# Fewer and later bias-row writes, half-size x loads for the squares, and shifted attention tasks in a hybrid decoder layer

## The chip, the cores and the metric

The kernel runs on one core of a Trainium2 chip. The metric is device microseconds (us) of one execution; the time before is the median of three runs.

## The reference

One layer: RMS norm of x (256 tokens by 4096), one input projection to 16384 columns, two token mixers, a gate on each, one output projection, a residual sum and a final RMS norm. With 256 tokens the attention has a single block per head, so it is plain causal attention with a bias that depends on the distance of query and key:

```python
u = rmsnorm(h, norm_gain)
q, k, v, z_a, hc, b_gate, c_gate, z_c = split(u @ w_in)      # 2048 columns each
logits = q @ k.T * 128 ** -0.5 + bias_tab[head, rel_bucket(i - j)]   # 16 heads x 128, j <= i
attn = softmax(logits) @ v * silu(z_a)
conv = b_gate * short_conv(c_gate * hc, conv_w) * silu(z_c)  # causal, width 3
h = h + concatenate([attn, conv]) @ w_out
out = rmsnorm(h, final_gain)
```

## The kernel before, in words

**The work in quads.** Weights stream through the core once. The 256 tokens are two halves of 128, columns are taken in pairs of 512-wide chunks, and the 4096 rows of a weight in 16 *quads* of 256 rows. A pair of chunks goes through 16 quads; there are 16 pairs for the input projection (p = 0 to 15) and four for the output projection (p = 16 to 19), so 320 quads. Each quad is one transfer of 1 MB into a buffer named raw. The 2 by 2 block product of a quad is done either in the usual way, with 8 block products (24 matmuls of 128x512), or, for quads 0, 2, 4, 6, 8 and 10, with 7 products of sums and differences (21 matmuls; "seven" quads below). Every operand is split into a high and a low part for accuracy: ACT casts `hi` (L472), DVE takes `lo` as the rest (L473), PE does hi x hi, hi x rest and lo x hi (L529 to L531). A seven quad also needs three sums on DVE (L461 to L463).

**Buffers and look-ahead.** raw has three buffers and is loaded two quads ahead (L435), all from SP's queue; hi and lo are rings of three, so that the splits run at most two units ahead of PE (a unit is half of a usual quad or a third of a seven quad).

**The first pair.** In p = 0 the x operands are also made. For each quad an x piece `xr` of 256 KB is loaded (L121), scaled with the norm's gain and split (L137 and L138, or for a seven quad L129, L113, L116 and L117). The order of quads in this pair (the list FIRST) has four usual quads first; then seven and usual quads alternate. In between lie three side jobs:

- `bias_rows` (called behind the third quad, i = 2): the bias table and a one-hot matrix are loaded (L188, L190), one matmul (L192) makes one row of 384 bias values per head, DVE copies it (L194), and one transfer (L195) writes each row 128 times to a scratch tensor in DRAM, `bias_d`.
- `squares` (i = 6 to 9): a quarter of x in row layout is loaded in two halves of 512 KB (L159), and ACT sums the squares (L160), for the RMS norm. The buffers have the tags "v" and "z".
- `token_scale` (i = 11) makes the factors of the norm, and `bias_load` fetches the bias tiles of heads 0 and 1. The rows of a bias tile are the same row shifted by one element each, which a stride of 383 over the copies in DRAM gives (L206, L208: two transfers of 128 partitions per head).

**End of a pair.** When the last seven quad of a pair is done, four of its sums are complete: `early` reads them out (L313 to L317, L580). After the last quad `two_done` (L328) writes the results: q and k after an even pair, v and z after an odd one.

**Attention tasks.** Groups of four heads are worked in between the block products of the following pairs. From the last seven quad of a pair on, the block products are counted, and a table (`tasks_of`) says after which count a task is emitted, and in which PSUM bank: `turn` (transposes of q and k, L216, copied by ACT, L218), `scores` (L223, L224, the bias added by DVE, L226, the softmax), `probs` (transposes, L240) in the odd pairs 1, 3, 5, 7; `values` and `mixed` in the even pairs 2 to 8; `conv` in pairs 10, 12, 14. `scores` of head h also calls `bias_load(h + 2)`, since there are two bias tiles. SP issues its DMAs strictly in the order in which they stand in its queue, and a DMA that has to wait for a buffer holds up all behind it. What stands in which place is decided by a scheduler; the order is the same in each execution.

Of the kernel before, what the change touches and what calls it, by code (L numbers as in the profile page):

```python
# [10 lines left out]
F32 = mybir.dt.float32  # L11
F32R = mybir.dt.float32r
BF16 = mybir.dt.bfloat16
AF = mybir.ActivationFunctionType
# [3 lines left out]
P = 128  # L18
S = 256
# [3 lines left out]
H = 16  # L23
HG = 4
NDP = 4
# [3 lines left out]
B = 512  # L29
# [3 lines left out]
RING = 3  # L33
LEAD = 2
BUCKETS = 32

EDGES = [16, 19, 21, 24, 27, 31, 35, 40, 46, 52, 59, 67, 77, 87, 99, 113]

# [21 lines left out]
def hymba_layer(ctx: ExitStack, tc: tile.TileContext, xT, xres, gain, w, convw, wout,  # L60
                relb, onehot, fgain, out):
    nc = tc.nc
    PSUM = bass.MemoryType.PSUM
    ps_ = ctx.enter_context(tc.tile_pool(name="ps", bufs=1, space=PSUM))
    dram = ctx.enter_context(tc.tile_pool(name="dram", bufs=1, space=bass.MemoryType.DRAM))
# [9 lines left out]
    sx = const.tile([P, 2, NDP], F32, name="sx")  # L75
    ss = const.tile([P, 2, 2 * NDP], F32, name="ss")
    const.tile([P, 8], F32, name="pad")
    bias_d = dram.tile([H, P, 384], F32, name="bias_d")
    m_d = dram.tile([NQ, P, 4 * P], F32, name="m_d")

    kt = ctx.enter_context(tc.tile_pool(name="kt", bufs=1, side="left"))
# [3 lines left out]
    pool = right.enter_context(tc.tile_pool(name="attn", bufs=1, side="right"))  # L85
    cur = {"pool": pool}

    def bank(n):
        return ps_.tile([P, 512], F32, name=f"p{n}")
# [62 lines left out]
            parts(dst, c[:, :4])  # L152


    def squares(p):
        for t in range(2):
            xq = pool.tile([P, 2, B], F32, name="xq", tag="vz"[t])
            xq = xq.rearrange("p n c -> p (n c)")
            nc.sync.dma_start(xq, xres[p][:, t * 2 * B:(t + 1) * 2 * B])  # L159
            nc.scalar.activation(xq, xq, AF.Square, accum_out=sx[:, t, p:p + 1])  # L160

    def rsqrt(dst, ps, n):

# [20 lines left out]
    def bias_rows():  # L184

        tab = pool.tile([BUCKETS + 1, H], F32, name="tab", tag="lg", bufs=2)
        nc.vector.memset(tab, MASKED)
        nc.sync.dma_start(tab[:BUCKETS], relb)  # L188
        oh = pool.tile([BUCKETS + 1, 384], F32, name="oh", tag="bt", bufs=2)
        nc.sync.dma_start(oh, onehot)  # L190
        ps = bank(5)
        nc.tensor.matmul(ps[:H, :384], tab, oh, start=True, stop=True)  # L192
        row = pool.tile([H, 384], F32, name="row", tag="lg", bufs=2)
        nc.vector.tensor_copy(row, ps[:H, :384])  # L194
        nc.sync.dma_start(bias_d, row[:, None, :].to_broadcast([H, P, 384]))  # L195


    V, Z, Q, K, QK, SM, PT, AM, BT, MT = [{} for _ in range(10)]

    def bias_load(h):  # L200
        if h >= H:
            return
        bt = BT[h] = pool.tile([P, 384], F32, name="bt", bufs=2)

        base = bias_d.offset + h * P * 384
        nc.sync.dma_start(bt[:, :S], bass.AP(tensor=bias_d.tensor, offset=base + 127,  # L206
                                             ap=[[383, P], [1, S]]))
        nc.sync.dma_start(bt[:, S:], bass.AP(tensor=bias_d.tensor, offset=base + 255,  # L208
                                             ap=[[383, P], [1, P]]))

    def turn(h, n):
        g, c = h // HG, (h % HG) * P
# [120 lines left out]
        two_done((Q[g], K[g]), (rQ, rT))  # L333

    def vz_end(g):
        V[g], Z[g] = (pool.tile([P, 2, B], F32, name=x) for x in "vz")
        two_done((V[g], Z[g]), (rT, rT))
        nc.scalar.activation(Z[g], Z[g], AF.Silu)

# [137 lines left out]
    def tasks_of(p):  # L477

        t = {}

        def put(at, f, *a):
            t.setdefault(at, []).append((f, a))
        if p < 8 and p % 2:
            for j, (at, banks) in enumerate(zip(((6, 10, 18), (9, 13, 21), (15, 19, 27), (18, 22, 30)),
                                                ((1, 7, 5), (6, 1, 7), (5, 6, 1), (7, 5, 6)))):
                for f, a_, n in zip((turn, scores, probs), at, banks):
                    put(a_, f, p // 2 * HG + j, n)
        elif 2 <= p <= 8:
            for j, (at, banks) in enumerate(zip(((6, 10), (10, 14), (14, 18), (18, 22)),
                                                ((1, 7), (6, 5), (1, 7), (6, 5)))):  # L490
                for f, a_, n in zip((values, mixed), at, banks):
                    put(a_, f, (p - 2) // 2 * HG + j, n)
        elif p in (10, 12, 14):
            for j in range(4):
                put(6 + 4 * j, conv, (p - 10) // 2 * 4 + j, (1, 6, 7, 5)[j])
        return t

    ENDERS = ([x for g in range(4) for x in ((qk_end, g), (vz_end, g))]
# [3 lines left out]
    for j, q in enumerate(OUT_FIRST):  # L502
        at = (15, (3, 5, 7, 8, 9, 10, 11, 12, 13, 14, 15)[j]) if j < 11 else (16, (0, 1, 2, 5, 6)[j - 11])
# [30 lines left out]
    for u, (n, kind, at, products) in enumerate(units):  # L534
        p, i, q = quads[n]
# [26 lines left out]
        if not end_of_quad:  # L562
            continue
        if p == 0:
            if 6 <= i < 6 + NDP:
                squares(i - 6)
            if i == 2:
                bias_rows()
            if i == 11:
                token_scale()  # L570
                bias_load(0)
                bias_load(1)
        if i == last_seven[p]:
            assert not tasks
            behind, tasks = 0, tasks_of(p)
# [7 lines left out]
        if (p, i) in M_AT:  # L583
            if not m_raw:
                m_raw[M_AT[p, i]] = m_load(M_AT[p, i])
            at = m_order.pop(0)
# [24 lines left out]
def _layout(x, norm_gain, w_in, conv_w, w_out, rel_bias, final_gain):  # L611
# [12 lines left out]
    for p in range(NDP):  # L624
# [3 lines left out]
    dist = 255 - np.arange(384)  # L628
    bucket = np.where(dist < 0, BUCKETS,
                      np.where(dist < 16, dist, 15 + np.searchsorted(EDGES, dist, side="right")))  # L630
    onehot = (bucket[None, :] == np.arange(BUCKETS + 1)[:, None]).astype(np.float32)
    return {
# [31 lines left out]
```

## Time and profile before

| | |
|---|---|
| median of 3 runs | 1776.4 us (1776.03 to 1777.66) |
| the profiled execution | 1777.55 us, of which 1775.8 us are the span from the first to the last instruction |
| mean granted PE clock | 0.989 |
| busy: PE, DVE, ACT | 1723.9 us (97%), 1458.5 us (82%), 1010.4 us (57%) |
| HBM read, written | 357.66 MB, 11.53 MB |

In a timeline row stand the start and the duration in us, the engine, the line, the operation, what it writes and reads, how many were merged and, in brackets, how long the engine was idle before and what ended that. A row of the waits has the waiting engine and line, then what it waited for, the total, the number of waits and the longest. A row of the windows gives the length of a stretch and each engine's busy time in it, then the granted PE clock, the DMA engines' share and the GB/s. A PE row's duration is the matmul's latency; matmuls overlap, and in steady state one starts every 0.23 us.

### The profile page before, as it was taken

The numbers are of one execution on the slowest core, as the hardware profiler recorded it, in microseconds if no ns is written. First come the engines' busy times: TensorE is split into PE (matmuls) and PEld (weight loads), VectorE is DVE, ScalarE is ACT, GpSimd is POOL, SyncE is SP. The second block draws the span as 40 slices with busy tenths as digits, with TensorE's granted clock in tenths as the row PEclk, the third lists the DMA queues.
The fourth block names the chain that finished last, engine by engine and source line by source line (L and its number), as shares of the span: only waits on it lengthen the run. The fifth ranks groups of instructions, "written<-read, shape, count | busy, mean of one in ns | idle before, by whom it ended". The sixth has DMA issues, their size and how long they took to land.

```text
span 1775.8 us, 20607 instructions
## 1 busy us (share of the span) xinstructions
PE 1723.9 (97%) x7698; PEld 1414.8 (80%) x7698; DVE 1458.5 (82%) x1591; ACT 1010.4 (57%) x1104; POOL 0.7 (0%) x6
## 2 busy tenths in 40 slices
PE   9489999999999999999999999999999999999996
PEld 7368888888888888888888888888888888788885
DVE  7498787878787878787878887887889999888886
ACT  6375665566556555755555564655555655555553
POOL 0000000000000000000000000000000000000000
PEclk9799999999999999999999999999999999999998
DMA  7875555555555555555645555555555776555563
GB/s 233 233 268 200 206 191 201 191 206 191 200 200 197 199 194 213 174 214 194 223 183 206 203 212 195 213 197 212 194 213 216 260 275 255 201 212 202 193 224 152
DMA packets 65264, 370.53 MB, mean 209 GB/s; under 512 B 7275, under 2 KB 13452, under 8 KB 24460
## 3 DMA queue, kind: packets, MB, share of 16 engines
q1 hardware_dynamic: 65164, 369.22, 58.0%
q8 instruction: 60, 0.98, 0.2%
q14 instruction: 40, 0.33, 0.1%
HBM read 357.66 MB, written 11.53 MB: 208 GB/s over the span
## 4 chain that ended last, share of the span: by engine, by line
PE 93%; DVE 2%; DMA 2%; ACT 1%; issue 1%; SPq 0%; DVEq 0%; ACTq 0%
PE p L531 30%; PE p L529 30%; PE p L530 30%; DMA raw<-in_w_dram 2%; DVE lo L473 1%; ACT hi L472 1%; PE p L216 0%; DMA xq<-in_xres_dram 0%; PE p L223 0%; PE p L240 0%; DVE hg L402 0%; ACT xq L160 0%; DVE hg L414 0%; PE p L251 0%; PE p L250 0%
## 5 line engine op out<-in xcount | busy, mean ns | idle before, releaser
L529 PE MATMUL p<-hi,k 128*128 128x512 f32 x2440 | 958.3, 394 | 32.1 <-ACT hi L472 31.7
L530 PE MATMUL p<-hi,k 128*128 128x512 f32 x2440 | 951.2, 390 | 0.0
L531 PE MATMUL p<-lo,k 128*128 128x512 f32 x2440 | 945.0, 391 | 3.8 <-DVE lo L473 3.3
L473 DVE TENSOR_TENSOR lo<-raw,hi 128x1024 fp32r<-128x1024 f32 (+2 forms) x524 | 692.0, 1333 | 138.5 <-ACT hi L472 137.0
L472 ACT CAST hi<-raw 128x1024 fp32r<-128x1024 f32 (+2 forms) x524 | 596.1, 1145 | 290.3 <-PE p L530 241.9
L529 PEld LDWEIGHTS p<-hi,k 128*128 128x128 f32 x2440 | 459.3, 188 | 132.1 <-ACT hi L472 38.7
L531 PEld LDWEIGHTS p<-lo,k 128*128 128x128 f32 x2440 | 458.2, 188 | 106.5 <-DVE lo L473 9.0
L530 PEld LDWEIGHTS p<-hi,k 128*128 128x128 f32 x2440 | 459.5, 188 | 93.6 <-issue 0.6
L472 ACT CAST hi<-sum 128x1024 fp32r<-128x1024 f32 x240 | 252.9, 1054 | 377.1 <-PE p L530 233.7
L473 DVE TENSOR_TENSOR lo<-sum,hi 128x1024 fp32r<-128x1024 f32 x240 | 292.7, 1219 | 105.7 <-ACT hi L472 105.4
L461 DVE TENSOR_TENSOR sum<-raw 128x1024 f32<-128x1024 f32 x120 | 146.3, 1219 | 6.4 <-DMA raw<-in_w_dram 4.6
L462 DVE TENSOR_TENSOR sum<-sum,raw 128x512 f32<-128x512 f32 x120 | 82.0, 683 | 0.3
L463 DVE TENSOR_TENSOR sum<-sum,raw 128x512 f32<-128x512 f32 x120 | 81.8, 682 | 0.1
L580 ACT ACTIVATE e<-e,rT 128x512 f32<-128x512 f32 x56 | 37.8, 715 | 2.0 <-DVE e L314 1.4
L138 DVE SCALAR_TENSOR_TENSOR k<-xr,g_sb,k 128x256 fp32r<-128x256 f32 x20 | 9.0, 479 | 26.1 <-ACT k L137 26.1
L137 ACT ACTIVATE k<-xr,g_sb 128x256 fp32r<-128x256 f32 x20 | 9.2, 500 | 25.4 <-DMA xr<-in_xT_dram 23.7
L116 ACT CAST k<-c 128x896 fp32r<-128x896 f32 (+1 forms) x22 | 17.3, 796 | 7.9 <-PE p L531 5.0
L117 DVE TENSOR_TENSOR k<-c,k 128x896 fp32r<-128x896 f32 (+1 forms) x22 | 19.7, 902 | 2.4 <-ACT k L116 2.4
L301 DVE SCALAR_TENSOR_TENSOR y<-p,cw,y 128x255 f32<-128x255 f32 (+1 forms) x32 | 15.4, 480 | 4.7 <-ACT y L299 4.3
L226 DVE TENSOR_TENSOR lg<-p,bt 128x384 f32<-128x384 f32 x16 | 8.9, 555 | 12.3 <-PE p L224 12.3
L231 ACT ACTIVATE lg<-lg,st 128x256 f32<-128x256 f32 (+1 forms) x32 | 14.3, 448 | 5.8 <-DVE st L230 5.5
L299 ACT ACTIVATE y<-p,cw 128x256 f32<-128x256 f32 x16 | 7.5, 470 | 12.0 <-PE p L297 12.0
(101 smaller groups left out, 425.5 us busy)
## 6 DMA issues: line engine op xcount, KB each, us to landing
raw<-in_w_dram SPq DMA_DIRECT2D x254, 1024.0 KB, 4.8
raw<-in_wout_dram SPq DMA_DIRECT2D x64, 1024.0 KB, 4.8
xr<-in_xT_dram SPq DMA_DIRECT2D x16, 256.0 KB, 7.8
xq<-in_xres_dram SPq DMA_DIRECT2D x8, 512.0 KB, 6.3
c<-m_d SPq DMA_DIRECT2D x16, 256.0 KB, 3.3
hg<-in_xres_dram SPq DMA_DIRECT2D x4, 1024.0 KB, 7.7
bias_d<-row SPq DMA_DIRECT2D x1, 3072.0 KB, 33.4
out_dram<-hg SPq DMA_DIRECT2D x6, 512.0 KB, 4.0
```

The lines of the kernel that those rows point to most:

```text
L116: nc.scalar.copy(dst[:, :, 0], c)
L117: nc.vector.tensor_tensor(dst[:, :, 1], c, dst[:, :, 0].bitcast(F32), ALU.subtract)
L301: nc.vector.scalar_tensor_tensor(y[:, i:], ps[:, :S - i], cw[:, k, 2 - i:3 - i], y[:, i:], op0=ALU.mult, op1=ALU.add)
L461: nc.vector.tensor_tensor(t[:, :2], raw[:, 1:3], raw[:, :1].to_broadcast([P, 2, B]), ALU.add)
L462: nc.vector.tensor_tensor(t[:, 2], t[:, 0], raw[:, 2], ALU.add)
L463: nc.vector.tensor_tensor(t[:, 3], t[:, 2], raw[:, 3], ALU.add)
L472: nc.scalar.copy(hi[:, c], src[:, c])
L473: nc.vector.tensor_tensor(lo[:, c], src[:, c], hi[:, c].bitcast(F32), ALU.subtract)
L529: nc.tensor.matmul(acc[b_], a, h_, start=s0, stop=False)
L530: nc.tensor.matmul(acc[b_], b, h_, start=False, stop=False)
L531: nc.tensor.matmul(acc[b_], a, l_, start=False, stop=s1)
L580: nc.scalar.activation(es[name], es[name], AF.Copy, scale=rows[c][:, t:t + 1])
```

## The change

Eight edits:

- The bias rows are written 32 times per head instead of 128 (0.75 MB in place of 3 MB). A bias tile of 128 rows is therefore put together from four strips of 32 rows: eight transfers per head instead of two.
- The matmul for the rows is emitted one quad earlier (i = 1). The write is a function of its own, `bias_store`, emitted in the next pair (p = 1, i = 0), and the first two bias tiles are fetched at p = 1, i = 4 and 5.
- `squares` does one half at a time, at i = 4 to 11.
- Its buffers have the tags "q" and "k".
- V and Z share their buffers with Q and K.
- `token_scale` comes at i = 12 instead of 11.
- `turn`, `scores`, `probs`, `values` and `mixed` are emitted 2 to 7 block products earlier, with other PSUM banks for some.
- `conv` starts 2 block products earlier and is spaced by 5 instead of 4.

```diff
+COPIES = 32
...
-    bias_d = dram.tile([H, P, 384], F32, name="bias_d")
+    bias_d = dram.tile([H, COPIES, 384], F32, name="bias_d")
...
-    def squares(p):
-        for t in range(2):
-            xq = pool.tile([P, 2, B], F32, name="xq", tag="vz"[t])
-            xq = xq.rearrange("p n c -> p (n c)")
-            nc.sync.dma_start(xq, xres[p][:, t * 2 * B:(t + 1) * 2 * B])
-            nc.scalar.activation(xq, xq, AF.Square, accum_out=sx[:, t, p:p + 1])
+    def squares(n):
+        p, t = divmod(n, 2)
+        xq = pool.tile([P, 2, B], F32, name="xq", tag="qk"[t]).rearrange("p n c -> p (n c)")
+        nc.sync.dma_start(xq, xres[p][:, t * 2 * B:(t + 1) * 2 * B])
+        nc.scalar.activation(xq, xq, AF.Square, accum_out=sx[:, t, p:p + 1])
...
-        nc.sync.dma_start(bias_d, row[:, None, :].to_broadcast([H, P, 384]))
+        return row
+
+    def bias_store(row):
+        nc.sync.dma_start(bias_d, row[:, None, :].to_broadcast([H, COPIES, 384]))
...
-        base = bias_d.offset + h * P * 384
-        nc.sync.dma_start(bt[:, :S], bass.AP(tensor=bias_d.tensor, offset=base + 127,
-                                             ap=[[383, P], [1, S]]))
-        nc.sync.dma_start(bt[:, S:], bass.AP(tensor=bias_d.tensor, offset=base + 255,
-                                             ap=[[383, P], [1, P]]))
+        base = bias_d.offset + h * COPIES * 384
+        for a in range(0, P, COPIES):
+            for c0, c1, at in ((0, S, P - 1), (S, 384, S - 1)):
+                nc.sync.dma_start(bt[a:a + COPIES, c0:c1],
+                                  bass.AP(tensor=bias_d.tensor, offset=base + at - a,
+                                          ap=[[383, COPIES], [1, c1 - c0]]))
...
-        V[g], Z[g] = (pool.tile([P, 2, B], F32, name=x) for x in "vz")
+        V[g], Z[g] = (pool.tile([P, 2, B], F32, name=x, tag=y) for x, y in ("vq", "zk"))
...
-            for j, (at, banks) in enumerate(zip(((6, 10, 18), (9, 13, 21), (15, 19, 27), (18, 22, 30)),
-                                                ((1, 7, 5), (6, 1, 7), (5, 6, 1), (7, 5, 6)))):
+            for j, (at, banks) in enumerate(zip(((4, 7, 14), (6, 10, 17), (9, 13, 20), (12, 16, 23)),
+                                                ((1, 7, 5), (6, 1, 6), (5, 7, 7), (6, 1, 5)))):
...
-            for j, (at, banks) in enumerate(zip(((6, 10), (10, 14), (14, 18), (18, 22)),
+            for j, (at, banks) in enumerate(zip(((4, 8), (8, 12), (12, 16), (16, 20)),
...
-                put(6 + 4 * j, conv, (p - 10) // 2 * 4 + j, (1, 6, 7, 5)[j])
+                put(4 + 5 * j, conv, (p - 10) // 2 * 4 + j, (1, 6, 7, 5)[j])
...
-            if 6 <= i < 6 + NDP:
-                squares(i - 6)
-            if i == 2:
-                bias_rows()
-            if i == 11:
+            if 4 <= i < 4 + 2 * NDP:
+                squares(i - 4)
+            if i == 1:
+                row = bias_rows()
+            if i == 12:
                 token_scale()
-                bias_load(0)
-                bias_load(1)
+        if p == 1 and i in (0, 4, 5):
+            if i:
+                bias_load(i - 4)
+            else:
+                bias_store(row)
```

Line numbers behind the edits grow by up to seven: L435 becomes L439, L473 becomes L477, L206 and L208 become L211.

**SP's queue in the first pair.** Here the write of the bias rows stands, before, between the loads of the sixth and the following quads; raw is a weight quad, xr its piece of x.

```order
L435 DMA raw<-in_w_dram 128x2048
L188 DMA tab<-in_relb_dram 32x16
L190 DMA oh<-in_onehot_dram 33x384
L121 DMA xr<-in_xT_dram 128x512
L435 DMA raw<-in_w_dram 128x2048
L195 DMA bias_d<-row 2048x1x384
L121 DMA xr<-in_xT_dram 128x512
L435 DMA raw<-in_w_dram 128x2048
```

In the changed kernel the same transfer, with a quarter of the rows, stands behind the last x pieces of the pair and the first quad of the next pair (the second of the two in "x2").

```order
L159 DMA xq<-in_xres_dram 128x1024
L122 DMA xr<-in_xT_dram 128x512
L439 DMA raw<-in_w_dram 128x2048 x2
L198 DMA bias_d<-row 512x1x384
L439 DMA raw<-in_w_dram 128x2048 x5
L211 DMA bt<-bias_d 32x256
```

So it has moved behind all x pieces and ten further weight quads, and is followed by weight quads alone.

**SP's queue in the tail of the second pair.** Before, the bias tiles of heads 2 to 5 (bt with its buffer's number) lie between four loads of weight quads.

```order
L435 DMA raw_1392<-in_w_dram 128x2048
L206 DMA bt_1416<-bias_d_75 128x256
L208 DMA bt_1416<-bias_d_75 128x128
L206 DMA bt_1443<-bias_d_75 128x256
L208 DMA bt_1443<-bias_d_75 128x128
L435 DMA raw_1468<-in_w_dram 128x2048
L206 DMA bt_1501<-bias_d_75 128x256
L208 DMA bt_1501<-bias_d_75 128x128
L435 DMA raw_1549<-in_w_dram 128x2048
L206 DMA bt_1534<-bias_d_75 128x256
L208 DMA bt_1534<-bias_d_75 128x128
L435 DMA raw_1595<-in_w_dram 128x2048
```

In the changed kernel all 32 transfers of the four tiles stand in one block; of each tile's eight, all but the first and the last are left out here.

```order
L439 DMA raw_1431<-in_w_dram 128x2048
L211 DMA bt_1413<-bias_d_75 32x256
...
L211 DMA bt_1413<-bias_d_75 32x128
L211 DMA bt_1455<-bias_d_75 32x256
...
L211 DMA bt_1455<-bias_d_75 32x128
L211 DMA bt_1495<-bias_d_75 32x256
...
L211 DMA bt_1495<-bias_d_75 32x128
L211 DMA bt_1530<-bias_d_75 32x256
...
L211 DMA bt_1530<-bias_d_75 32x128
L439 DMA raw_1545<-in_w_dram 128x2048
L439 DMA raw_1597<-in_w_dram 128x2048
```

The first quad of the next pair (raw_1468 before, raw_1545 now) has moved from behind two bias tiles to behind four.

**DVE around the norm's factors, late in the first pair.** Before, the sum over the squares (L177) stands behind all the splits of a seven quad; k is an x operand.

```order
L462 TENSOR_TENSOR sum<-sum,raw 128x512
L473 TENSOR_TENSOR lo<-sum,hi 128x1024
L463 TENSOR_TENSOR sum<-sum,raw 128x512
L177 TENSOR_REDUCE s2x<-sx 128x2
L138 SCALAR_TENSOR_TENSOR k_760<-xr,g_sb,k_760 128x2x128
L166 TENSOR_SCALAR rs_v<-s2x 128x2
```

Now it stands right behind the first step of a seven quad's x operand (L114, L113 before).

```order
L114 TENSOR_TENSOR c<-c 128x128
L177 TENSOR_REDUCE s2x<-sx 128x2
L114 TENSOR_TENSOR c<-c 128x128
L166 TENSOR_SCALAR rs_v<-s2x 128x2
L114 TENSOR_TENSOR c<-c 128x128
L465 TENSOR_TENSOR sum<-raw 128x1024
L168 RECIPROCAL rT<-rs_s 128x2
```

It has moved one to two quads later, ahead of that quad's sums and splits.

## The prediction, made before the result was known

> **What bounds the kernel now.** I read the waits first, over the whole span, then again from 140 us on. A row is the waiting engine and line, what it waited for, the total in us, the number of waits and the longest.
>
> ```profile
> PE p L529 <- ACT hi L472: 31.7, 8, 25.1
> PE p L531 <- DVE lo L473: 3.3, 5, 1.5
> ```
>
> From 140 us to the end only this is left:
>
> ```profile
> PE p L531 <- DVE lo L473: 1.7, 3, 1.1
> PE p L529 <- ACT hi L472: 0.3, 1, 0.3
> ```
>
> So from the second pair of chunks on PE waits 2.0 us in 1636; nothing that gets faster there can shorten the run, and only a new wait can lengthen it. What can be won lies in the first pair, nearly all of it in one wait of 25.1 us. The timeline around it, engine by engine:
>
> ```profile
> 45.14 0.39 PE L531 MATMUL p<-lo,k 128*128 128x512 f32 x1
> 70.63 0.80 PE L529 MATMUL p<-hi,k 128*128 128x512 f32 x1 [25.10 <-ACT hi L472]
> ...
> 41.99 2.50 DVE L473 TENSOR_TENSOR lo<-sum,hi 128x1024 fp32r<-128x1024 f32 x2
> 67.49 0.88 DVE L138 SCALAR_TENSOR_TENSOR k<-xr,g_sb,k 128x256 fp32r<-128x256 f32 x2 [23.00 <-ACT k L137]
> ...
> 66.94 0.91 ACT L137 ACTIVATE k<-xr,g_sb 128x256 fp32r<-128x256 f32 x2 [23.72 <-DMA xr<-in_xT_dram]
> ```
>
> All three engines stand still, and the end of the chain is an x piece that does not arrive until 66.9 us. SP's timeline and the list of DMA issues (size, us to landing) say why:
>
> ```profile
> 23.57 0.35 SPq L435 DMA_DIRECT2D raw<-in_w_dram  x1
> 32.07 0.69 SPq L195 DMA_DIRECT2D bias_d<-row  x1
> 32.81 9.75 SPq L121 DMA_DIRECT2D xr<-in_xT_dram  x1
> 42.66 4.32 SPq L435 DMA_DIRECT2D raw<-in_w_dram  x1
> ...
> bias_d<-row SPq DMA_DIRECT2D x1, 3072.0 KB, 33.4
> ```
>
> Between 23.57 and 32.07 SP issues nothing, since the bias write waits for its row. Then the write takes 33.4 us, and the x piece issued 0.7 us behind it lands as the write ends: whatever stands behind in the queue waits for it. So the stall is the bias write's, both its wait and its length.
>
> **Which engine sets the pace without it.** The windows give each engine's busy time before the stall, in it, from it to the end of the first pair, and in one clean stretch of two quads (a usual and a seven one):
>
> ```profile
> 22.30:44.50 22.20, 22.20 (x98) 17.54 (x96) 21.19 (x28) 13.39 (x16) 0.00 (x0) 1.00 0.68 143
> 44.60:67.40 22.80, 0.93 (x5) 0.46 (x3) 0.00 (x0) 0.46 (x2) 0.00 (x0) 0.62 0.90 136
> 67.40:131.20 63.80, 53.64 (x213) 39.81 (x213) 56.81 (x81) 50.49 (x70) 0.00 (x0) 0.95 0.79 291
> ...
> 82.99:94.43 11.44, 9.73 (x41) 7.73 (x42) 11.31 (x15) 10.24 (x15) 0.00 (x0) 1.00 0.88 296
> ```
>
> The third column is PE, the fifth (after PE's weight loads) DVE. In the clean stretch DVE is busy 11.31 of 11.44 us and PE 9.73: late in the first pair, where the x operands are made as well, DVE is the limit. The pair ends for DVE where it reads out the last sums:
>
> ```profile
> 131.22 0.74 DVE L328 SCALAR_TENSOR_TENSOR k<-p,rT,e 128x512 f32<-128x512 f32 x1
> ```
>
> **The change part by part: the stall.** The write no longer stands ahead of x pieces or of quads that are short. What is late next is DVE. Its last split before the stall ends at 41.99 + 2.50 = 44.49 us, and from there to L328 it has 56.81 us of work, which the change leaves as it is. Before, it was idle 63.80 − 56.81 = 7.0 us beside that. The clean stretch has 0.13 us of idle time per 11.44, some 0.6 over the rest of the pair; those are the bounds. I take 3.5: the restart goes, but the norm's factors now come at a worse place. There DVE waits for the last square and then for a root, and ACT has these between its casts:
>
> ```profile
> L160 ACT ACTIVATE xq<-xq x8: 1045/1054/1062, 79.8 to 103.5; 128x1024 f32<-128x1024 f32 x8
> ...
> 107.44 1.28 ACT L167 ACT_TABLE_LOAD   x1
> ```
>
> One square of 1.05 us and one table load of 1.28 in DVE's way are some 2 us, and 1.5 remain for small waits on ACT.
>
> The row copy (L194) moves one quad up, ahead of the splits that feed PE. On DVE's clock it would stand at about 26 us; PE's order has the row's matmul 18 matmuls earlier than before, and the matmul ran at 30.6 us:
>
> ```profile
> L192 PE MATMUL p<-oh,tab x2: 482/488/493, 30.6 to 31.0; 33*16 33x384 f32 x2
> L194 DVE COPY row<-p x1: 545/545/545, 31.5 to 31.5; 16x384 f32<-16x384 f32 x1
> ```
>
> With 22.20/98 = 0.2265 us per matmul it comes at 30.6 − 4.1 = 26.5 us and is done by 27.4. DVE may wait between nothing and 1.3 us; before it waited hardly at all. I take 0.5.
>
> Sum for L328: 44.49 + 56.81 + 3.5 + 0.5 = 105.3 us, against 131.22: a gain of 25.9 us.
>
> **The squares.** Before, SP waits for a buffer of the squares, with weight loads behind it:
>
> ```profile
> SPq L159 <- ACT xq L160: 19.9, 6, 7.6
> ```
>
> Half by half over eight quads, each load waits for the square two before it, a quad or more ago. That wait goes, but its value is already in DVE's idle time above; alone it is 0. The move to q's and k's buffers waits for nothing (Q and K are first written at the end of the pair), nor does V on Q's buffer, whose transposes are done 20 block products earlier, or Q on V's.
>
> **The write at its new place.** SP reaches it right behind the quad with which the second pair begins. A quarter of 33.4 is 8.4 us. Behind it stands the second quad of that pair, which SP may issue only when the last but one quad of the first pair is split, and which is cast only after two more quads, the read-outs and L328, 13.5 us of DVE time later by before's rows (from the end of the last but one quad's last split at 121.50 to that second quad's):
>
> ```profile
> 120.28 1.22 DVE L473 TENSOR_TENSOR lo<-sum,hi 128x1024 fp32r<-128x1024 f32 x1
> 134.99 2.35 DVE L473 TENSOR_TENSOR lo<-raw,hi 128x1024 fp32r<-128x1024 f32 x2
> ```
>
> The write's 8.4 us, most of it over by then, and the quad's own 4.8 (row below) fit into that. Cost 0; if the cover were gone, up to 8.4.
>
> **The eight loads per head.** Here instructions are added: 96 more transfers, in the tails of pairs 1, 3, 5 and 7. Rows of before (least, median and largest ns of the issue, then landings, then SP in the tail of the second pair, and the cast that needs the first quad of the third):
>
> ```profile
> L206 SPq DMA_DIRECT2D bt<-bias_d x16: 319/320/548, 101.0 to 727.0; - x16
> L208 SPq DMA_DIRECT2D bt<-bias_d x16: 320/427/1054, 101.6 to 727.4; - x16
> ...
> bt<-bias_d SPq DMA_DIRECT2D x16, 128.0 KB, 2.1
> bt<-bias_d SPq DMA_DIRECT2D x16, 64.0 KB, 1.9
> raw<-in_w_dram SPq DMA_DIRECT2D x254, 1024.0 KB, 4.8
> ...
> 196.13 0.33 SPq L206 DMA_DIRECT2D bt<-bias_d  x1
> 196.50 0.43 SPq L208 DMA_DIRECT2D bt<-bias_d  x1
> 200.70 0.33 SPq L435 DMA_DIRECT2D raw<-in_w_dram  x1
> ...
> 195.54 0.56 DVE L226 TENSOR_TENSOR lg<-p,bt 128x384 f32<-128x384 f32 x1 [0.24 <-PE p L224]
> 208.16 0.55 DVE L226 TENSOR_TENSOR lg<-p,bt 128x384 f32<-128x384 f32 x1
> ...
> 214.70 1.48 ACT L472 CAST hi<-raw 128x1536 fp32r<-128x1536 f32 x1 [0.73 <-PE p L530]
> ```
>
> All in before's clock. The first add of a group of heads comes 9 matmuls (2.0 us) earlier, at 193.5, and frees its bias tile at 194.1. Before, the four adds lay 12.6 us apart over 36 matmuls, 8.2 us; 4.4 are task work. Now they lie 27 matmuls apart: 6.1 + 4.4 = 10.5 us. So the last tile is free at 204.6, and its eight issues at 0.43 us end at 208.1; counted as a chain of 32 from 194.1 they end at 207.9. The quad behind, issued at 200.70 before, goes at about 208.1 and lands at 212.9, 1.8 us ahead of the cast at 214.70. DVE's sums of that quad stand behind the splits of the pair, so they hold up nothing. Cost 0, but with thin cover: at 0.32 us per issue there are 2.7 us to spare; at 0.55 the chain ends at 211.7, 1.8 us late. Three tails (1, 3, 5) have all 32 issues, the fourth only 16. I put 1 us into the sum.
>
> The third and fourth head need their tiles within the group: 194.1 + 16 × 0.43 + 2.1 = 203.1, against the add at 204.0. Also covered.
>
> **Tasks earlier, other banks, conv spacing.** Same instructions; PE showed no wait on a task. The tightest step is the copy of the transposes before the scores: 9 matmuls and 4 transposes cover a copy on ACT. Cost 0, bounds −1 and +3 us over all pairs (the 2.0 us of waits there, and a third of a us for each of the tasks' ten pairs).
>
> **PE's clock.** In the stall the granted clock falls to 0.62, and once more after the end of the first pair:
>
> ```profile
> 131.20:136.20 5.00, 4.84 (x14) 3.63 (x15) 5.00 (x8) 2.26 (x3) 0.00 (x0) 0.66 0.56 202
> ```
>
> There 14 matmuls start where 22 would fit, 1.8 us; with the stall's own slow start DVE sets the pace anyway. I take 0, with 1.8 as a possible extra gain. The Trainium skill (TensorE: Matmul & The Clock Gate, Part 1: The HAM clock gate) says that the clock halves after about 3.4 us of idle PE and returns after as much work. By that rule the stall's end would cost PE some 1.7 us as an estimate, and the time would be 1750 instead of 1752; the trace agrees on the fall, but has DVE behind in that stretch.
>
> **Sum.** 25.9 − 1 = 24.9 us off. The profiled execution took 1777.55, 1.15 above the median of 1776.4; the sum gives 1752.7 against the one and 1751.5 against the other: 1752.
>
> **Rivals.** *The issues hold the weight quads (partly).* At 0.5 to 0.65 us per issue the chain ends 210 to 215, up to 5 us late per tail, three times: 15 us, so 1752 to 1767, say 1762. For it: the longest issue of before, 1.054 us. Against: the medians.
>
> *The quarter write still blocks.* If SP reaches it while a quad is short, 8.4 us of stall come back: 1760. Against it: the 13.5 us above.
>
> *Slower: the same queue at its worst.* With every issue at 1.054 us the chain ends at 194.1 + 33.7 = 227.8, and the quad is 17.9 us late in each of three tails: 54 − 25 = 29 us slower, 1805. It turns the sign from 0.75 us per issue on (8.3 us late in each tail). Only one row of 32 is near it.
>
> *Slower: the pieces land one after another.* If the eight strips of a head run in series, 8 × 1.9 = 15.2 us per head, the fourth head's tile lands at 194.1 + 30.4 = 224.5, 20 us after its add, in four tails: 80 − 25, 1831. Against: the two transfers issued 0.37 us apart at 196 land in about 2 us each from their own issue, so they overlap. The Trainium skill (SBUF — State Buffer, "Can I just issue two DMAs to hit both halves?") says that transfers to different partitions serialize on the same DMA engines, and speaks for one transfer over 128 partitions; no run here shows small ones do.
>
> *No gain.* The write's place changes but DVE's idle time grows by as much, from ACT or the DMA engines: about 1776. Against: the clean stretch, at 0.88 DMA share, runs with squares in it.
>
> **How the numbers follow.** Forecast 0.74, partly held quads 0.10, quarter write 0.06, no gain 0.03, slower by slow issues 0.05, by strips in series 0.02. The forecast's own range: with 0.6 us of DVE idle, no wait at L194 and the clock's 1.8 the gain is 131.22 − 101.9 + 1.8 = 31; with 7.0, 1.3 and 3 × 1.2 us of late quads it is 131.22 − 109.6 − 3.6 = 18. That is 1745 to 1758; with part of the two milder rivals 1746 to 1761. A measurement of this kernel can tell about 0.2%, 3.6 us, from no change. Faster 0.90, same 0.03, slower 0.07.
>
> **What would show it.** Right: no PE wait above 3 us in the first pair; L328 first at 103 to 109 us; DVE busy over 90% between 45 us and there; the bias write landing in some 8 us with no x piece behind it; strip issues at about 0.4 us; no wait of ACT or DVE for raw after the first pair. Wrong: PE idle in the tails of pairs 1, 3 and 5 with ACT or DVE waiting for raw, strips that land later than 3 us, or L328 past 115.

## The result, and the profile after

The changed kernel takes 1750.17 us (median of 4 runs, 1748.89 to 1751.07) against 1777.03 us for the kernel before beside it (1776.03 to 1778.91): ratio 0.9847, 95% interval 0.983 to 0.9864. The forecast was 1752.0, with a range of 1746 to 1761. The two profiled executions took 1777.55 and 1750.56 us.

PE's waits after, over the whole span (the two largest groups), have none above 2.3 us:

```profile
PE p L535 <- DVE lo L477: 3.3, 4, 1.5
PE p L533 <- ACT hi L476: 2.8, 4, 2.3
```

The wait of 25.1 us is gone and none took its place. The windows of the changed kernel (PE, PE's weight loads, DVE, ACT, POOL, granted clock, DMA share, GB/s) run up to 44.5 us, from there to the read-outs, and over the short slow clock behind them:

```profile
22.30:44.50 22.20, 22.20 (x96) 17.35 (x95) 19.62 (x27) 16.74 (x23) 0.00 (x0) 1.00 0.72 272
44.50:104.00 59.50, 55.32 (x228) 41.66 (x228) 58.83 (x86) 49.08 (x66) 0.00 (x0) 0.99 0.80 276
104.00:110.00 6.00, 6.00 (x23) 4.65 (x22) 5.97 (x7) 2.47 (x3) 0.00 (x0) 0.82 0.36 123
```

DVE is busy for 58.83 of 59.50 us: 0.7 us idle, where before it stood idle for 7.0 of the 63.8 us behind the stall. Two waits of DVE that the prediction spoke of, for the row's matmul and for the norm's root, and the read-out that ends the pair for DVE (131.22 before) are now these:

```profile
28.65 0.55 DVE L194 COPY row<-p 16x384 f32<-16x384 f32 x1 [1.33 <-PE p L192]
...
84.93 0.17 DVE L168 RECIPROCAL rT<-rs_s 128x2 f32<-128x2 f32 x1 [0.55 <-ACT rs_s L167]
...
102.51 0.74 DVE L332 SCALAR_TENSOR_TENSOR k<-p,rT,e 128x512 f32<-128x512 f32 x1
```

SP's queue around the write (L198), then in the tail of p = 1, and the two operations that need the quad behind the strips:

```profile
77.10 5.66 SPq L439 DMA_DIRECT2D raw<-in_w_dram  x2
82.81 0.70 SPq L198 DMA_DIRECT2D bias_d<-row  x1
...
165.34 16.03 SPq L211 DMA_DIRECT2D bt<-bias_d  x32
...
186.50 1.23 DVE L465 TENSOR_TENSOR sum<-raw 128x1024 f32<-128x1024 f32 x1 [0.92 <-DMA raw<-in_w_dram]
...
186.57 1.49 ACT L476 CAST hi<-raw 128x1536 fp32r<-128x1536 f32 x1 [2.25 <-DMA raw<-in_w_dram]
```

The chain of 32 strips takes 16.03 us, 0.50 from one to the next, not the 0.43 of the sum; it ends at 181.4, and the quad that goes then is there at 186.5, when DVE begins on it. ACT and DVE wait for it, PE does not. A single issue did not become longer: it takes 419 ns at the median (first row below: least, median, largest). The rest of the 0.50 lies between the issues, in waits of SP for the adds that free the bias tiles (second row: 5.4 us in four waits, over the whole span), and in one issue of 1.217 us. The landings of the strips overlap, as the list of DMA issues shows (median us to landing in the last column):

```profile
L211 SPq DMA_DIRECT2D bt<-bias_d x128: 302/419/1217, 113.2 to 702.2; - x128
...
SPq L211 <- DVE lg L230: 5.4, 4, 1.3
...
bt<-bias_d SPq DMA_DIRECT2D x64, 32.0 KB, 1.8
bt<-bias_d SPq DMA_DIRECT2D x64, 16.0 KB, 1.8
```

**A finer measure than the time.** The start-up differs from execution to execution, also of one and the same program: the 16th matmul of the block products begins between 10.11 and 13.42 us in the 14 traces of this study, and at 12.28 and 13.18 us in the two of the changed kernel. So the traces are compared from there on, by the starts of three matmuls: the 16th (a), the 49th of p = 1 (b) and the first of p = 8 (c). In the trace after they are

```profile
12.28 0.40 PE L533 MATMUL p<-hi,k 128*128 128x512 f32 x1
...
113.35 0.39 PE L533 MATMUL p<-hi,k 128*128 128x512 f32 x1
...
721.33 0.39 PE L533 MATMUL p<-hi,k 128*128 128x512 f32 x1
```

and before

```profile
11.05 0.39 PE L529 MATMUL p<-hi,k 128*128 128x512 f32 x1
...
142.08 0.39 PE L529 MATMUL p<-hi,k 128*128 128x512 f32 x1
...
748.34 0.39 PE L529 MATMUL p<-hi,k 128*128 128x512 f32 x1
```

From a to b (the first pair and its end) that is 131.03 us before and 101.07 after; from b to c (the pairs with the heads) 606.26 and 607.98. The part behind c is alike in all kernels, within 1.1 us. The program after was run again beside other kernels and gave 101.10 and 608.03, so this measure repeats to some 0.05 us. All kernels:

| kernel | us, median | ratio to before, 95% interval | a to b | b to c |
|---|---|---|---|---|
| before | 1777.0 to 1778.5 | | 131.03 | 606.26 |
| after | 1750.17 | 0.983 to 0.9864 | 101.07 | 607.98 |
| after, again | 1750.57 | 0.9833 to 0.986 | 101.10 | 608.03 |
| a1: 32 copies alone | 1759.78 | 0.9881 to 0.9911 | 110.32 | 606.84 |
| a2: later alone | 1767.49 | 0.9926 to 0.9956 | 120.10 | 606.26 |
| a3: both bias edits alone | 1753.86 | 0.9851 to 0.9884 | 105.18 | 606.70 |
| a4: all but the bias edits | 1774.79 | 0.9972 to 0.9991 | 127.75 | 606.45 |
| b1: after, 16 copies | 1790.49 | 1.0055 to 1.0082 | 99.94 | 649.07 |
| b2: after, 64 copies | 1748.50 | 0.9821 to 0.9847 | 101.11 | 606.18 |
| b3: after, strips from POOL | 1752.69 | 0.9846 to 0.9873 | 101.35 | 610.03 |
| b4: after, squares in pairs | 1751.16 | 0.9834 to 0.9861 | 102.07 | 607.99 |
| b5: after, old task table | 1749.48 | 0.9822 to 0.9849 | 101.10 | 606.28 |
| c1: b5, sums on POOL | 1753.42 | 0.9848 to 0.9875 | 106.45 | 606.28 |
| c2: after, 24 DVE operations more | 1758.27 | 0.987 to 0.9903 | 108.06 | 608.61 |

### The profile page after: what moved, and what is told of

It reads as the page before. It is cut to its first block, busy times and chain, and to the rows that moved or that the text cites. A ratio compares the mean times of both kernels' runs of the same rounds, so it can differ in the third digit from the quotient of the medians.

```text
span 1748.8 us, 20735 instructions
## 1 busy us (share of the span) xinstructions
PE 1723.5 (99%) x7698; PEld 1413.3 (81%) x7698; DVE 1456.7 (83%) x1591; ACT 1005.3 (57%) x1104; POOL 0.7 (0%) x6
## 4 chain that ended last, share of the span: by engine, by line
PE 91%; DVE 5%; ACT 2%; issue 1%; DMA 0%; SPq 0%; DVEq 0%; ACTq 0%
PE p L533 30%; PE p L535 30%; PE p L534 30%; DVE lo L477 2%; ACT hi L476 1%; PE p L220 0%; PE p L227 0%; DVE sum L466 0%; DVE sum L465 0%; DVE sum L467 0%; DVE k L118 0%; PE p L244 0%; DVE hg L406 0%; DMA raw<-in_w_dram 0%; DVE hg L418 0%
## 5 line engine op out<-in xcount | busy, mean ns | idle before, releaser
L477 DVE TENSOR_TENSOR lo<-raw,hi 128x1024 fp32r<-128x1024 f32 (+2 forms) x524 | 692.1, 1334 | 144.4 <-ACT hi L476 141.5
L477 DVE TENSOR_TENSOR lo<-sum,hi 128x1024 fp32r<-128x1024 f32 x240 | 292.8, 1220 | 103.0 <-ACT hi L476 102.7
L402 ACT ACTIVATE e<-hg 128x512 f32<-128x512 f32 x16 | 10.0, 625 | 7.0 <-DVE hg L400 6.7
L114 DVE TENSOR_TENSOR c<-c 128x128 f32<-128x128 f32 x48 | 11.9, 280 | 1.3 <-DMA c<-m_d 1.2
```

What stands on the lines that cost most here:

```text
L477: nc.vector.tensor_tensor(lo[:, c], src[:, c], hi[:, c].bitcast(F32), ALU.subtract)
```

## The experiments

The theory was the prediction's: the bias write blocked SP's queue in order, by its length and by its wait; without it DVE sets the pace of the first pair; the price is the issue of the strips.

**a1: 32 copies alone.** The edit on the kernel before:

```diff
+COPIES = 32
-        nc.sync.dma_start(bias_d, row[:, None, :].to_broadcast([H, P, 384]))
+        nc.sync.dma_start(bias_d, row[:, None, :].to_broadcast([H, COPIES, 384]))
```

with the strip loads of the change, and everything in its old place.

> The kernel before with 32 copies instead of 128 (and eight strip loads per head); the write stays at its old place, behind the sixth quad. Theory (the write blocks the in-order queue by its length and by its wait for the row): the write takes a quarter of 33.4, 8.4 us, and SP's 8 us of waiting for the row at 24 to 32 us stay. The x piece behind it lands at about 32 + 8.4 + 3 = 43.5 us, nearly when ACT asks for it (43.2), so the longest PE wait falls from 25.1 us to under 8 us, and L328 first comes at 108 to 115 us: 1755 to 1762 us. Rival (the length hardly matters, the place does): the stall stays over 15 us and the time over 1766.

Measured 1759.78; a to b is 20.7 us shorter than before. The write lands in 9.7 us instead of 33.4, 23.7 us sooner. SP's queue, the write, PE's wait where the stall was, and the longest wait of PE:

```profile
33.75 0.69 SPq L196 DMA_DIRECT2D bias_d<-row  x1
...
bias_d<-row SPq DMA_DIRECT2D x1, 768.0 KB, 9.7
...
48.89 0.51 PE L531 MATMUL p<-hi,k 128*128 128x512 f32 x1 [1.66 <-ACT hi L474]
...
77.38 14.57 SPq L209 DMA_DIRECT2D bt<-bias_d  x16
...
104.82 0.80 PE L531 MATMUL p<-hi,k 128*128 128x512 f32 x1 [4.36 <-ACT hi L474]
```

The time, the longest wait and the first read-out (112.34 us) are as expected; the write is 9.7 us long instead of 8.4. Of the stall's 25.1 us only 1.66 are left in its place. The 4.36 us are another wait: the chain there runs over the read-outs of the four sums by ACT and DVE, and between 85 and 112 us PE, ACT and DVE show no wait for a DMA. At the old place the 16 strips of the first two heads stand ahead of the last x piece for 14.57 us; that this costs anything is not shown.

**a2: later alone.** The kernel before with `bias_store` at p = 1, i = 0 and the first loads at i = 4 and 5, 128 copies.

```diff
-                bias_load(0)
-                bias_load(1)
+        if p == 1 and i in (0, 4, 5):
+            if i:
+                bias_load(i - 4)
+            else:
+                bias_store(row)
```

> The kernel before with the write and the first bias loads moved to the second pair alone; still 128 copies, 3 MB. Theory: the 33.4 us of blocking go along with the write; DVE's cover there is 13.5 us, so some 15 to 20 us of the stall come back in the second pair, as a wait of PE for a split that waits for raw: 1766 to 1772 us. Rival (the place alone does it, the write is hidden there): no wait above 3 us in the second pair and 1750 to 1755 us.

Measured 1767.49, within the theory's range. The write, its landing, and who waits:

```profile
79.72 0.68 SPq L198 DMA_DIRECT2D bias_d<-row  x1
...
bias_d<-row SPq DMA_DIRECT2D x1, 3072.0 KB, 35.3
...
117.63 1.22 DVE L464 TENSOR_TENSOR sum<-raw 128x1024 f32<-128x1024 f32 x1 [14.07 <-DMA raw<-in_w_dram]
...
119.23 0.80 PE L532 MATMUL p<-hi,k 128*128 128x512 f32 x1 [17.83 <-ACT hi L475]
```

The write takes as long as before, and the stall moves with it, shortened from 25.1 to 17.8 us by the cover. So the place alone does not do it, and the rival of this run is refuted.

**a3: both bias edits alone.** a1 and a2 together.

> The kernel before with both bias edits (32 copies, later), and nothing else: squares in pairs in the old buffers, the old task table, V and Z in their own buffers. Theory (these two are the whole gain): 1750 to 1755 us; SP's waits for the squares' buffers (19.9 us before) stay and cost at most 3 us. Rival (the squares or the tasks carry a part of the gain): 1756 us or more.

Measured 1753.86: a to b is 25.85 us shorter, of the 29.96 that the whole change brings. DVE's timeline at the end of its first pair, and PE behind it:

```profile
98.93 0.75 DVE L333 SCALAR_TENSOR_TENSOR q<-p,rQ,e 128x512 f32<-128x512 f32 x1 [0.38 <-PE p L536]
...
101.58 1.21 DVE L466 TENSOR_TENSOR sum<-raw 128x1024 f32<-128x1024 f32 x1
...
101.35 0.50 PE L534 MATMUL p<-hi,k 128*128 128x512 f32 x1 [1.85 <-ACT hi L477]
...
105.24 1.22 PE L536 MATMUL p<-lo,k 128*128 128x512 f32 x2 [2.67 <-DVE lo L478]
```

Here DVE does all four read-outs ahead of the sums of the next seven quad, and PE waits 1.85 and 2.67 us for those; in the changed kernel (the row of 102.51 us above) the sums and two splits come first. By time the theory's range holds; by the traces the other edits carry 4.1 us.

**a4: all but the bias edits.** The changed kernel with 128 copies, written at i = 2, and the first bias loads behind `token_scale`.

> The changed kernel with both bias edits undone: 128 copies written in the first pair as before; the halves of the squares, buffers, tasks and conv spacing stay changed. Theory (everything else is worth nothing): 1774 to 1780 us, the PE wait of some 25 us is back. Rival (the rest carries a part): under 1773 us.

Measured 1774.79, ratio 0.9972 to 0.9991: the stall is back at its full size,

```profile
69.79 0.80 PE L528 MATMUL p<-hi,k 128*128 128x512 f32 x1 [25.18 <-ACT hi L471]
```

and yet a to b is 3.3 us shorter than before. The range holds, but "worth nothing" is not right: some 3 us. The order of DVE's work at the end of the pair is that of before here, with sums and two splits ahead of the read-outs. From its first subtraction for an x operand to the first read-out DVE has the same 108 operations and stands idle for 28.4 us instead of 30.9, so most of these 3 us are small waits of DVE.

**b4: squares in pairs again.** The changed kernel with the old shape of the squares at i = 6 to 9, in the new buffers.

```diff
-            if 4 <= i < 4 + 2 * NDP:
-                squares(i - 4)
+            if 6 <= i < 6 + NDP:
+                squares(i - 6)
```

> The changed kernel with the squares again in pairs at the sixth to ninth place, in the new buffers. The bias edits alone came out at 1753.9 us and the changed kernel without them 3 us under the kernel before, so 3 to 4 us lie in the other edits. Theory A (they lie in the halves of the squares: SP's waits for their buffers and two squares at a stroke on ACT): 1752.5 to 1755 us, with over 15 us of SP waiting for a square. Theory B (they lie in the order at the end of the first pair, set by other edits): 1749 to 1751.5 us. What was predicted was that the squares are worth nothing alone.

Measured 1751.16, B's range; a to b is 1.0 us longer than after. By the traces the halves are worth 1 us (by the times alone it would be within the noise), and the other 3 us of the difference to a3 lie in the edits that are left: V's and Z's buffers, the buffers of the squares, the place of `token_scale`, the row's matmul a quad earlier. PE's waits in a3 stand where DVE's order at the end of the pair is another one; which of these edits sets that order was not tried one by one.

**b5: the old task table.** The changed kernel with the old numbers and banks in `tasks_of`.

> The changed kernel with the old table of tasks, old banks and old conv spacing. The first pair is the same as in the changed kernel. Theory (as predicted, the tasks are worth nothing by themselves; what is lost in pairs 2, 4 and 6 is the order around the read-outs that the new table gives): pairs 2, 4 and 6 gain 0.6 us each, 1748 to 1750.5 us. Rival (the earlier tasks give the strips their cover: without them the quad behind the strips is late): PE waits in three tails of 1 us or more, and 1753 to 1760 us.

Measured 1749.48. a to b is the same (101.10); b to c is 606.28, the 1.7 us came back. With the old table SP's queue in the tail reads 16 strips, a quad, 16 strips; the adds now wait for strips, without cost for PE, whose two waits behind 140 us come to 1.9 us:

```profile
PE p L535 <- DVE lo L477: 1.5, 2, 1.1
PE p L533 <- DVE b L332: 0.4, 1, 0.4
...
  DMA bt<-bias_d: 5.2, 4
```

But the theory's cause does not follow: a4 has the new table with two loads per head, and loses nothing either (606.45). So the loss needs both, the new table and eight strips per head, which together put 32 strips in one piece ahead of a quad.

**b2: 64 copies.** `COPIES = 64` in the changed kernel: 1.5 MB written, four loads per head.

> The changed kernel with 64 copies: 1024 rows written, four strip loads per head. Theory (a write at the new place is free up to the cover of 13.5 us, strips cost their issues): the write takes 16.8 us, so up to 3 us of stall in the second pair (the write of 33.4 us left 17.8 us of PE wait there, a cover of 15.6); the chains on SP halve to 8 us and the 0.6 us of pairs 2, 4 and 6 may come back: 1749 to 1754 us, a longest PE wait of 1 to 3.5 us at the second quad of the second pair. Rival (the cover is used up by the 0.75 MB write already): 8 us of stall more, 1757 us or above.

Measured 1748.50. In the tail the strips, now of 32 and 64 KB, stand in two groups of eight; in the second pair the write of 1.5 MB is just covered: ACT waits 3.40 us for raw, and PE 0.97 for the split behind it:

```profile
164.85 5.52 SPq L211 DMA_DIRECT2D bt<-bias_d  x8
...
104.37 2.00 ACT L476 CAST hi<-raw 128x1024 fp32r<-128x1024 f32 x2 [3.40 <-DMA raw<-in_w_dram]
...
105.88 0.73 PE L535 MATMUL p<-lo,k 128*128 128x512 f32 x2 [0.97 <-DVE lo L477]
```

a to b is as in the changed kernel (101.11), and b to c is 606.18, so the 1.8 us are back. It is the fastest kernel here and beats the kernel before; its interval overlaps that of the changed kernel run beside it (0.9833 to 0.986), so that it beats this one too rests on the traces, not on the times.

**b1: 16 copies.** `COPIES = 16`: the issues doubled, 64 in a tail.

> The changed kernel with 16 copies: 256 rows written (4 us), 16 strip loads per head instead of eight, so chains of 64 issues on SP in the tails of pairs 1, 3 and 5, and 32 in that of pair 7. Theory (the issues' time on SP is the price of fewer copies, with thin cover): at 0.50 us, as the changed kernel shows, a chain takes 32 us instead of 16, the quad behind it goes 16 us later, of which a few us are covered; PE waits 8 to 14 us in each of three tails, and the time is 1775 to 1795 us. Rival (strips and quads overlap enough, or the scheduler puts the quads ahead): no PE wait over 3 us in those tails and 1748 to 1755 us.

Measured 1790.49, slower than the kernel before. In the tail of p = 1 SP, ACT and PE read

```profile
162.93 31.15 SPq L211 DMA_DIRECT2D bt<-bias_d  x64
...
199.06 1.47 ACT L476 CAST hi<-raw 128x1536 fp32r<-128x1536 f32 x1 [9.00 <-DMA raw<-in_w_dram]
...
200.58 0.79 PE L533 MATMUL p<-hi,k 128*128 128x512 f32 x1 [11.05 <-ACT hi L476]
```

0.49 us from one issue to the next, 15.1 us more than with 32 strips, of which 11 reach PE in this one wait; b to c is 42.8 us longer than before, some 14 for each of the three tails. This is the prediction's slower rival, brought about by the number of issues instead of by a longer issue. With 0.6 us lost per tail at 32 strips and over 10 at 64, the change stands right at the edge of its cover.

**b3: strips from POOL's queue.** The changed kernel with one word changed.

```diff
-                nc.sync.dma_start(bt[a:a + COPIES, c0:c1],
+                nc.gpsimd.dma_start(bt[a:a + COPIES, c0:c1],
```

> The changed kernel with the strip loads issued from POOL's queue instead of SP's. Theory (the 0.6 us that the changed kernel loses in each of pairs 2, 4 and 6 comes from the raw quad that stands behind 32 strips): these 1.8 us come back, 1747 to 1749 us, and no wait of ACT or DVE for raw in those tails. Rival 1 (the loss is one of order alone): within 1 us of the changed kernel. Rival 2 (POOL issues more slowly, over 1 us each): the third and fourth head's tiles come late, the adds wait over 5 us per group, and the time is above 1755.

Measured 1752.69, none of the three times; in kind it is rival 2, at half its price per issue. The first two groups of eight on POOL, and the third add, which now waits for its tile:

```profile
165.58 7.81 POOL L211 DMA_DIRECT2D bt<-bias_d  x16 [61.46 <-DVE lg L230]
...
178.18 0.56 DVE L230 TENSOR_TENSOR lg<-p,bt 128x384 f32<-128x384 f32 x1 [2.54 <-DMA bt<-bias_d]
...
PE p L244 <- ACT lg L235: 2.4, 4, 0.8
```

An issue takes 0.50 us there. No cast waits for a quad any more, but the adds wait for their tiles, and through the softmax so do PE's `probs`. b to c is 2.1 us longer than after, so the strips cost time on either of the two queues that were tried.

**c1: the seven quads' x sums on POOL.** b5 with `nc.gpsimd` in `sums_of` for the x operands.

> The changed kernel with the old task table (1749.5 us) and the 24 sums for the x operands of the seven quads (L114, 0.27 us each on DVE) moved from DVE to POOL. Theory (DVE sets the pace of the first pair behind 45 us): 20 of them, 5 us of DVE's work, go from that stretch, and the second pair begins 2 to 5 us earlier: 1744.5 to 1747.5 us. Rival (ACT, the DMA engines or PE hold the first pair as well, or POOL's sums come late): within 1.5 us of 1749.5 or slower, with DVE idle by over 4 us between 45 and 100 us.

Measured 1753.42: slower, and the expectation that less work on DVE shortens the pair failed. ACT's longest group of waits in the first pair, and the group of DVE's x splits between 44.5 and 100 us (behind the first bar: busy us, mean ns of one), with the sums on POOL:

```profile
ACT k L117 <- POOL c L114: 9.1, 3, 3.4
...
L139 DVE SCALAR_TENSOR_TENSOR k<-xr,g_sb,k 128x256 fp32r<-128x256 f32 x10 | 5.9, 617 | 0.0
```

and the same group in b5, without them:

```profile
L139 DVE SCALAR_TENSOR_TENSOR k<-xr,g_sb,k 128x256 fp32r<-128x256 f32 x10 | 4.7, 469 | 0.0
```

POOL's four sums stand in a chain that ACT waits for, 9.1 us in three waits, and DVE's x splits beside them grow. The Trainium skill (SBUF — State Buffer, Who interferes with whom) says that a DVE operation with two inputs in SBUF and a POOL operation that reads SBUF share a port, and that the one that comes second is blocked; the longer splits agree with that, and no run here shows the port itself. So c1 changes two things beside DVE's work, and tells nothing of DVE's pace; c2 was made for that.

**c2: 24 idle operations more on DVE.**

```diff
+            for a, b in ((0, 2), (1, 0), (4, 1), (3, 5)):
+                nc.vector.tensor_tensor(junk, c[:, a], c[:, b], ALU.subtract)
```

> The changed kernel with 24 idle operations added on DVE in the first pair: each of the six seven quads there gets four more subtractions of 128x128 (0.27 us each) whose result nobody reads, behind the operands' split and so not in their chain. Theory (behind 45 us DVE sets the pace of the first pair): the 20 of them in that stretch add 4 to 5.5 us of work, and the second pair begins 3.5 to 6 us later: 1754 to 1757 us. Rival (DVE is full but PE, ACT or the DMA engines hold the pair as much, or DVE's share has slack): under 1.5 us later, 1750 to 1752 us.

Measured 1758.27, 7.7 us above the changed kernel beside it; a to b is 7.0 us longer. The windows from 44.5 us on, after (run again) and with the 24 operations:

```profile
44.50:100.00 55.50, 53.02 (x223) 40.64 (x222) 54.82 (x81) 46.36 (x62) 0.00 (x0) 1.00 0.85 291
```

```profile
44.50:100.00 55.50, 47.29 (x191) 34.31 (x191) 54.20 (x93) 42.95 (x59) 0.00 (x0) 1.00 0.79 270
...
L136 DVE TENSOR_TENSOR junk<-c x24: 259/273/285, 25.3 to 90.5; 128x128 f32<-128x128 f32 x24
```

DVE was full and stays full, and PE gets through 191 matmuls instead of 223. From DVE's first subtraction for an x operand to the first read-out its busy time grows by 5.0 us (the profile has its neighbouring operations overlap a little, so 24 of 0.273 us add less than 6.6) and its idle time by 1.3; the last 0.6 come behind the read-out. So the added work appears in full: DVE sets the pace. The time is above the 1754 to 1757 us expected. Eight of the 24 operations stand ahead of 44.5 us, not four as the expectation had it, and they cost as well; and the order at the end of the pair changed, with one PE wait of 5.0 us, to which the remaining 2 us belong as far as is known.

## Why the prediction was right, step by step

- **The stall and its cause: right.** a1 undoes its length and a2 its place: 20.7 and 10.9 us; together (a3) 25.85, against 25.9 in the sum. That the two numbers agree is partly chance, since a3's read-outs come in another order than after. What SP's wait of 8 us for the row cost by itself no run shows apart.
- **DVE sets the pace behind it: right** (58.83 of 59.50 us, and c2). The term of DVE's idle time was too large: 0.7 us measured where 3.5 were taken and 0.6 was the lower bound. Of the 2 us taken for the last square and the root only the root's 0.55 showed. The wait at L194 was 1.33 us, just above its bound of 1.3 and 0.8 more than taken, but a wait of 0.88 for ACT, which before stood at 27.76 us, is gone. The work was not quite "as it is" either: the same 108 operations, from the first subtraction for an x operand to the first read-out, keep DVE busy for 75.81 us instead of 76.87, which the sum did not have and no run explains. With 2.8 for the idle time, 0.8 lost at L194, 0.9 won at ACT and 1.1 of work this comes to 4.0 of the 4.1 us that the sum had too little.
- **L328 at 103 to 109: it came at 102.51**, half a us ahead of these bounds although the start-up was 1.23 us slower. That is 90.23 us behind the 16th matmul against 120.17 before, 29.9 us earlier.
- **The squares, and "alone it is 0": failed, and so did the 0 for the rest.** SP's wait for the squares' buffers went, as predicted (19.9 us before, none after, 13.9 in b4), and the halves are worth 1.0 us (b4). What is left beside the bias edits makes about 3 us. In a3 these show as PE waits with DVE in another order at the end of the first pair; a4 keeps the old order and gains 3.3 us all the same, mostly from small waits of DVE. Whether the two are the same 3 us stays open. The tasks' table is worth 0 in the first pair (b5).
- **The write at its new place, cost 0: right.** The cover is even longer than the 13.5 us worked out: 35.3 us of write left 17.8 us of stall in a2, so 17.5 are covered, and twice the change's write costs PE 0.97 us at one place and nothing over the pair in b2. The write itself is longer than the 8.4 us of the sum: the trace of the changed kernel does not give its landing, but 0.75 MB took 9.7 us in a1, 10.4 in a3 and, at the new place, 10.7 in c2.
- **The strips, 1 us: the long chain right, its size small, and the way to PE another.** The chain goes at 0.50 us per strip, not 0.43, since the sum left out the spaces and waits between issues. The cast waits 2.25 us for the quad behind it, where the sum had the quad 1.8 us early, and DVE waits 0.9; so the sign "no wait of ACT or DVE for raw" did not come. PE does not wait there. Still 0.6 us is lost in each of p = 2, 4 and 6, 1.7 together. Read at p = 2, the loss comes when ACT waits for a sum that DVE makes late,

```profile
204.28 1.05 ACT L476 CAST hi<-sum 128x1024 fp32r<-128x1024 f32 x1 [3.29 <-DVE sum L467]
...
205.38 0.50 PE L533 MATMUL p<-hi,k 128*128 128x512 f32 x1 [0.16 <-ACT hi L476]
```

  so it reaches PE through DVE's order, not at the late quad itself. Whether the lateness or the order that the scheduler chose for so many issues is its cause stays open: in b2, b3, b4 and b5 the two change together or not at all.
- **Landing of strips: right.** 1.8 us each while 32 of them go 0.50 us apart, so their landings overlap; 64 of them go 0.49 us apart. Whether their data moved one after another the landings do not tell. The Trainium skill (SBUF — State Buffer, "Can I just issue two DMAs to hit both halves?") speaks for one transfer over 128 partitions, since others serialize on the same engines; here the measurement decides, and what many small ones cost here is SP's time to issue them, not their landing.
- **PE's clock, 0: right.** In the first two pairs the slow clock comes once, 0.82 over 104 to 110 us, as before behind the end of the pair; the one inside the stall went with it. The Trainium skill (TensorE: Matmul & The Clock Gate, Part 1: The HAM clock gate) would have made up to an estimated 1.7 us of that. The second run of the changed kernel settles it for the end of the pair: there the clock stays full,

```profile
100.00:112.00 12.00, 9.31 (x36) 6.07 (x35) 11.97 (x14) 7.07 (x8) 0.00 (x0) 1.00 0.36 121
```

  and a to b is 101.10 us against 101.07 with the slow clock. For the slow clock at the end of the stall no run shows it apart.

The whole: 29.96 us in the first pair, 1.72 lost up to p = 8, and 1.23 lost because this execution started up more slowly (12.28 against 11.05 us at the 16th matmul), 27.0; the profiled executions differ by 26.99. The sum said 24.9: 4.1 too little in the first pair, 0.7 too little for the strips, and a start-up that it could not know. The first miss is up and the other two are down, so that the total came within 2 us of the sum is partly luck.

## What to carry to other kernels

In this queue, which issues in order, a long DMA that waited for its data held up everything behind it, so make such a DMA short and put it where the work that is behind it is covered; doing only one of the two left 5 or 15 us of 26 unclaimed here. When a transfer is cut into more pieces, count the issues in the queue they share, at the price they have back to back with the waits between them, and compare the chain with the cover of the next transfer: here 16 issues cost nothing, 32 in one piece cost 0.6 us per tail and 32 in two pieces nothing, 64 cost over 10. Where a change moves order as well as work, try the parts one at a time before a remainder of a few us is put down to any of them.

## What was not expected of the hardware

- Issues on SP come further apart in a row than one of them takes: 0.50 us each over 32 and 0.49 over 64, although one takes 0.42 at the median, as before (0.32 and 0.43). With 64 copies, strips of 32 and 64 KB, one takes 0.60 at the median, and eight took 5.52 us, 0.69 each. On POOL's queue one takes 0.50 us.
- DVE's operations grew while POOL computed: the x split from 469 to 617 ns. POOL's own subtraction of 128x128 took 905 ns at the median against 284 on DVE:

```profile
L114 POOL TENSOR_TENSOR c<-c x24: 458/905/4030, 23.0 to 86.7; 128x128 f32<-128x128 f32 x24
L114 DVE TENSOR_TENSOR c<-c x24: 280/284/293, 1345.7 to 1418.7; 128x128 f32<-128x128 f32 x24
```

- The start-up moves by 3.3 us over the 14 traces (10.11 to 13.42 us at the 16th matmul), and by 0.9 between two of one program; behind it, these two agree to 0.05 us.
